# One decoder block on one core: the seven products of a 2x2 split in a form with four weight sums, made on DVE

## The chip, the cores and the metric

The kernel runs on one core of a Trainium2 chip. The metric is the device time of one execution in microseconds. Engines are named as in the profile: PE (TensorE), DVE (VectorE), ACT (ScalarE), POOL (GpSimd), and SP, which here only issues DMAs.

## The reference, cut to what matters

One layer of a hybrid decoder. The input is normalised, projected by one wide matrix, mixed by two causal token mixers, gated, projected back, added to the input and normalised again.

```python
u = _rmsnorm(h, norm_w)                              # 512 x 2048
proj = jnp.matmul(u, w_in.astype(jnp.float32))       # 2048 x 20528
(ml_q, ml_k, ml_v, ml_o, ml_z, ml_i, ml_f,
 dn_qkv, dn_z, dn_b, dn_a, gate_a, gate_b) = jnp.split(proj, idx, axis=-1)
...
h_a = h_a * jax.nn.sigmoid(ml_o) * jax.nn.silu(ml_z)
...
y_a = jnp.matmul(h_a, w_out[:ML_WIDTH])
y_b = jnp.matmul(h_b, w_out[ML_WIDTH:])
return jax.nn.sigmoid(gate_a) * y_a + jax.nn.sigmoid(gate_b) * y_b
```

The change touches only the part of `proj` for gate_b (columns 2048 to 4095 of the gates), ml_v, ml_z and ml_o: 8192 of the columns of `w_in`. All is float32.

## The kernel before, in words

**Precision.** Every float32 operand of a matmul is split into a high part (a cast to fp32r on ACT, `split_hi`, L130) and a low part (source minus high part on DVE, `split_lo`, L133). A product is three matmuls: high x high, high x low, low x high.

**Order of the work.** PE's order is the order of the program text; the other engines' instructions are put in order by the tile framework's scheduler, with priorities (`tc.high_priority`, `urgent`, `behind`). First u is normalised and transposed into `uh`, `ul` (16 tiles of 128 rows by 512 tokens). Then come the projections of one block of ML_Q and one of ML_K (`proj_cm`), then the stage of seven products, then narrow gate blocks (`narrow_gates`, whose first matmuls are L338 to L341), the units of the two mixers, wide gate blocks, and the output projection (L1217 to L1219).

**The stage of seven products.** `SEVEN` lists eight blocks: two of gates ("g"), two of ml_v ("v"), four of ml_z with ml_o ("z"). A block is a product of u with two column blocks of 512, c1 and c2. Along the 2048 rows of the weights, two neighbouring tiles of 128 form the halves of a 2x2 split, as the two halves of the tokens (256 each) and the two column blocks do; instead of eight quarter products seven are formed of sums (a scheme of Strassen's kind). Each product runs over KH = 8 pairs of tiles i, for two token tiles t, with three matmuls of 128 x 512: 7 x 8 x 2 x 3 = 336 matmuls per block.

Before, `seven` calls `group` twice. Group A does three products per i, group B four. Both add over i in banks of PSUM and at i = 7 add or copy the result into the four quarters X11, X12, X21, X22 of the SBUF tile `X` (L487, L490, L497, L498); `SINK[kind]` then applies tanh and the gates and stores from X (g_d, L531 to L538, for z blocks). `gates`, started after the stage, loads small gate rows and lets PE transpose them (L569) after POOL has cleared masks (L623) in a pool that takes over the stage's SBUF space.

**Weights.** `rplan` and `pplan` list raw tiles and prepared tiles. A raw tile is one DMA of 256 KB by SP (L216); `sum_next` makes a sum of two raw tiles (L228; the list names POOL for four of the five sums per i, DVE for one); `split_next` splits it. `next_w` is called ahead of each step of PE and keeps raw tiles, sums and splits a few steps ahead. The raw tiles of group A are loaded again for group B.

**Sums of u.** `u_sums`, started with the projection of ML_K, forms the sums of u for each i: POOL adds high and low parts (L453), then two sums (L455, L456), DVE one (L458); all are split (L462, L463) into `s5`, `s1` and `s6`.

Of the kernel before, what the change touches and what calls it, by code (L numbers as in the profile page):

```python
# [8 lines left out]
F32 = mybir.dt.float32  # L9
# [20 lines left out]
NEXTRA = 5  # L30
SUMAHEAD = 5
# [27 lines left out]
def hybrid_body(  # L59
# [80 lines left out]

    rplan, pplan = [], []

    def add_raw(w, c, k, nk, n, extra=False):
        rplan.append((w[k * P:(k + nk) * P, c:c + n], nk, n, extra))
        return len(rplan) - 1

    def add_plain(key, *raw):
        pplan.append((key, (add_raw(*raw),), None, None))

    for c in (ML_Q, ML_K):  # L150
        for k in range(0, KT, KP):
            add_plain(("i", c, k), w_in, c, k, KP, NB)
    nx = [0]

    def extra_raw(c, k):
        nx[0] += 1
        return add_raw(w_in, c, k, 1, NO, (nx[0] - 1) % (NRAW + NEXTRA) < NEXTRA)

    for kind, c1, c2 in SEVEN:
        for i in range(KH):  # L160
            r11, r22 = extra_raw(c1, 2 * i), extra_raw(c2, 2 * i + 1)
            for m, (rs_, op) in enumerate((((r11,), None), ((r22,), None), ((r11, r22), ALU.add))):
                pplan.append((("A", c1, i, m), rs_, op, G))
        for i in range(KH):
            r11, r12 = extra_raw(c1, 2 * i), extra_raw(c2, 2 * i)
            r21, r22 = extra_raw(c1, 2 * i + 1), extra_raw(c2, 2 * i + 1)
            for m, (rs_, op, e) in enumerate((((r21, r11), ALU.subtract, G), ((r12, r22), ALU.subtract, V),
                                              ((r11, r12), ALU.add, G), ((r21, r22), ALU.add, G))):
                pplan.append((("B", c1, i, m), rs_, op, e))
    def add_gates(blocks):  # L170
        for b in blocks:
            for k in range(0, KT, KP):
                add_plain(("i", GATE + b * NB, k), w_in, GATE + b * NB, k, KP, NB)

    add_gates(range(GFIRST))
    for kind, p in UNITS:
        cols = (DN_K, DN_Q, DN_V, DN_Z) if kind == "d" else (ML_Q, ML_K)
        for c in cols:
            for k in range(0, KT, KP):
                add_plain(("i", c + p * NB, k), w_in, c + p * NB, k, KP, NB)  # L180
    add_gates(range(GFIRST, GNARROW))
    for c in range(GATE + GNARROW * NB, GATE + GEND * NO, NO):
        for k in range(KT):
            add_plain(("w", c, k), w_in, c, k, 1, NO)
    for nb in range(D // NO):
        for k in range(2 * KT):
            add_plain(("o", nb * NO, k), w_out, nb * NO, k, 1, NO)

    left = [0] * len(rplan)
    for _, rs_, _, _ in pplan:  # L190
        for r in rs_:
            left[r] += 1
    raws, sums, parts = [], [], []
    held = {False: [], True: []}
    used = [0]
    extra_pool = []

    def may_load():
        r = len(raws)
        if r == len(rplan):  # L200
            return False
        extra = rplan[r][3]
        n = NEXTRA if extra else NRAW
        return len(held[extra]) < n or left[held[extra][-n]] == 0

    def load_raw():
        assert may_load()
        r = len(raws)
        src, nk, n, extra = rplan[r]
        held[extra].append(r)  # L210
        with tc.high_priority(offset=2 * PRIO if r > RAHEAD else 0):
            if extra:
                raw = extra_pool[0].tile([P, nk, n], F32, tag="wr2", name="wr", bufs=NEXTRA)
            else:
                raw = wp.tile([P, nk, n], F32, tag="wr", name="wr", bufs=NRAW)
            nc.sync.dma_start(raw, src.rearrange("(k p) n -> p k n", p=P))  # L216
        raws.append(raw)

    def sum_next():
        key, rs_, op, e = pplan[len(sums)]  # L220
        while len(raws) <= max(rs_):
            load_raw()
        if op is None:
            sums.append(None)
            return
        with tc.high_priority(offset=2 * PRIO):
            t = wp.tile([P, 1, NO], F32, tag="tg", name="ws", bufs=3)
            e.tensor_tensor(out=t, in0=raws[rs_[0]], in1=raws[rs_[1]], op=op)  # L228
        for r in rs_:
            left[r] -= 1  # L230
        sums.append(t)

    def split_next():
        i = len(parts)
        while len(sums) <= i:
            sum_next()
        src = sums[i]
        if src is None:
            r = pplan[i][1][0]
            src = raws[r]  # L240
            left[r] -= 1
        _, nk, n, _ = rplan[pplan[i][1][0]]
        with tc.high_priority(offset=2 * PRIO if i > SAHEAD else 0):
            hi = wp.tile([P, nk, n], F32R, tag="wh", name="wh", bufs=NSPL)
            lo = wp.tile([P, nk, n], F32R, tag="wl", name="wl", bufs=NSPL)
            with ExitStack() as first:
                if not parts:
                    first.enter_context(behind("V"))
                    first.enter_context(behind("A"))
                split_hi(hi, src)  # L250
                split_lo(lo, src, hi)
        parts.append((hi, lo))

    def next_w(*key):
# [1029 lines left out]
```

## Time and profile before

| | before |
|---|---|
| timed runs | 2368.11, 2370.42, 2370.58 us, median 2370.42 |
| profiled execution | 2375.3 us, its span 2373.5 us |
| mean granted TensorE clock | 0.991 |
| busy: PE, DVE, ACT, POOL | 2250.5, 1623.2, 924.4, 669.9 us |
| stage of seven products | first matmul at 86.0 us, first matmul behind it at 796.0 us |
| HBM read, written | 303.80 MB, 51.68 MB |

A row of a group reads: line, engine, operation, output and inputs by the program's names, shapes, count; then busy time, mean ns of one, and the idle time of the engine just ahead of them with what ended it. A row of the timeline reads: start, duration, engine, line, operation, and in brackets the idle time ahead of it with what ended it; "x4" means four merged instructions. A row of busy time by stretch gives the stretch, its length, and for each engine the busy time and the number of instructions, then the granted clock, the busy share of the DMA engines and their GB/s. "ps" is a PSUM bank of the stage, "wr" a raw tile, "ws" a sum of weights, "wh" and "wl" the split parts.

### The profile page before, as it was taken

To read this page: it belongs to the slowest core of one execution; us is meant where nothing else is said; L and a number is where in the kernel's file an instruction comes from. 1 tells how busy PE (TensorE), PEld (TensorE's weight loads), DVE (VectorE), ACT (ScalarE), POOL (GpSimd) and SP (SyncE) were. 2 spreads that over 40 slices of the span, in tenths; PEclk is the share of its full clock that TensorE was granted. 3 is DMA by queue.
4 is the path that set the end of the run, shared out by engine and by line. 5 is a ranking of instruction groups with operands and counts; after the bars stand their busy time and mean duration, and the time that the engine had idled before them with its cause. 6 is when DMAs were issued, how large, how long until landed. Compare 5 with 4: busy or idle time off the path is not lost.

```text
span 2373.5 us, 33466 instructions
## 1 busy us (share of the span) xinstructions
PE 2250.5 (95%) x11455; PEld 1853.5 (78%) x11455; DVE 1623.2 (68%) x2739; ACT 924.4 (39%) x1902; POOL 669.9 (28%) x573
## 2 busy tenths in 40 slices
PE   6799899999999799999999999999999999999998
PEld 5577677777777698888878888888888997888886
DVE  4998988899999748683677648683778434444334
ACT  4345444344444334433433334343443324322222
POOL 0864664564575313020221112110311000010010
PEclk9999999999999899999999999999999999999999
DMA  4345555555555465574665656574665458634433
GB/s 146 98 146 177 181 156 174 180 156 150 164 154 159 143 169 135 134 182 109 162 145 138 173 127 152 133 189 116 158 138 140 125 164 253 194 114 124 124 116 129
DMA packets 484141, 357.72 MB, mean 151 GB/s; under 512 B 236705, under 2 KB 391554, under 8 KB 483970
## 3 DMA queue, kind: packets, MB, share of 16 engines
q1 hardware_dynamic: 400258, 329.06, 50.0%
q10 hardware_dynamic: 83712, 26.52, 4.5%
q8 instruction: 90, 1.47, 0.2%
q14 instruction: 81, 0.66, 0.1%
HBM read 303.80 MB, written 51.68 MB: 150 GB/s over the span
## 4 chain that ended last, share of the span: by engine, by line
PE 57%; issue 14%; POOL 9%; DVE 8%; DMA 5%; ACT 1%; SPq 1%; ACTq 0%; POOLq 0%; DVEq 0%
PE pj L323 10%; PE pj L324 9%; PE pj L325 9%; POOL ws L228 9%; PE py L1217 5%; PE py L1219 5%; PE py L1218 5%; DVE wl L133 3%; DVE X L490 2%; PE pjt L338 2%; PE pjt L340 2%; PE pjt L341 2%; DMA wr<-in_w_in_dram 2%; PE ps L476 1%; PE ps L477 1%
## 5 line engine op out<-in xcount | busy, mean ns | idle before, releaser
L133 DVE TENSOR_TENSOR wl<-wr,wh 128x512 fp32r<-128x512 f32 x640 | 487.6, 765 | 426.6 <-ACT wh L130 407.2
L130 ACT CAST wh<-wr 128x512 fp32r<-128x512 f32 x640 | 395.6, 620 | 853.1 <-PE pj L324 345.6
L323 PE MATMUL pj<-uh,wh 128*128 128x512 f32 x1280 | 529.7, 414 | 2.2 <-ACT yp L675 1.2
L325 PE MATMUL pj<-uh,wl 128*128 128x512 f32 x1280 | 501.5, 392 | 3.1 <-DVE wl L133 3.1
L324 PE MATMUL pj<-ul,wh 128*128 128x512 f32 x1280 | 500.6, 391 | 0.3 <-DVE ul L405 0.3
L228 POOL TENSOR_TENSOR ws<-wr 128x512 f32<-128x512 f32 x256 | 410.8, 1624 | 274.2 <-DVE wl L133 266.0
L133 DVE TENSOR_TENSOR wl<-ws,wh 128x512 fp32r<-128x512 f32 x320 | 335.6, 1076 | 31.8 <-ACT wh L130 24.6
L130 ACT CAST wh<-ws 128x512 fp32r<-128x512 f32 x320 | 198.8, 621 | 279.8 <-POOL ws L228 204.4
L325 PEld LDWEIGHTS pj<-uh,wl 128*128 128x128 f32 x1280 | 240.6, 188 | 56.5 <-DVE wl L133 4.0
L323 PEld LDWEIGHTS pj<-uh,wh 128*128 128x128 f32 x1280 | 241.5, 189 | 48.9 <-ACT uh L404 1.7
L324 PEld LDWEIGHTS pj<-ul,wh 128*128 128x128 f32 x1280 | 241.7, 189 | 43.9 <-DVE ul L405 0.8
L1217 PE MATMUL py<-wh,hh 128*128 128x512 f32 x512 | 200.7, 392 | 4.2 <-ACT tgw L1177 4.2
L1218 PE MATMUL py<-wl,hh 128*128 128x512 f32 x512 | 200.1, 391 | 0.0
L1219 PE MATMUL py<-wh,hl 128*128 128x512 f32 x512 | 200.1, 391 | 0.0
L477 PE MATMUL ps<-wl,s6h 128*128 128x512 f32 x256 | 106.1, 414 | 23.6 <-DVE wl L133 23.6
L477 PE MATMUL ps<-wl,s5h 128*128 128x512 f32 x256 | 104.1, 406 | 24.4 <-DVE wl L133 24.4
L1217 PEld LDWEIGHTS py<-wh,hh 128*128 128x128 f32 x512 | 96.7, 189 | 25.6 <-ACT tgw L1177 5.8
L1241 POOL TENSOR_TENSOR hf<-hf,fw 128x512 f32<-128x512 f32 x12 | 18.6, 1572 | 336.2 <-DMA wr<-in_w_out_dram 173.2
L1219 PEld LDWEIGHTS py<-wh,hl 128*128 128x128 f32 x512 | 96.7, 189 | 20.3
L1218 PEld LDWEIGHTS py<-wl,hh 128*128 128x128 f32 x512 | 96.8, 189 | 20.0
L338 PE MATMUL pjt<-wh,uh 128*128 128x256 f32 x384 | 112.1, 292 | 0.0
L340 PE MATMUL pjt<-wl,uh 128*128 128x256 f32 x384 | 109.6, 285 | 1.2 <-DVE wl L133 1.2
(282 smaller groups left out, 3823.8 us busy)
## 6 DMA issues: line engine op xcount, KB each, us to landing
wr<-in_w_in_dram SPq DMA_DIRECT2D x768, 256.0 KB, 3.0
wr<-in_w_out_dram SPq DMA_DIRECT2D x128, 256.0 KB, 2.9
tgl<-tg_d SPq DMA_DIRECT2D x32, 256.0 KB, 3.6
xt<-in_x_dram SPq DMA_DIRECT2D x8, 512.0 KB, 8.2
tg_d<-X ACTq DMA_DIRECT2D x16, 256.0 KB, 3.5
v_d<-X ACTq DMA_DIRECT2D x16, 256.0 KB, 5.1
g_d<-X ACTq DMA_DIRECT2D x16, 256.0 KB, 2.4
v<-v_d SPq DMA_DIRECT2D x8, 512.0 KB, 6.0
```

Of the source, the lines that this page charges most:

```text
L130: newest["A"] = A.copy(hi, src).ins
L133: newest["V"] = V.tensor_tensor(out=lo, in0=src, in1=hi.bitcast(F32), op=ALU.subtract).ins
L228: e.tensor_tensor(out=t, in0=raws[rs_[0]], in1=raws[rs_[1]], op=op)
L323: T.matmul(ps[j], hi[:, k, wsl], uh[:, kt, :], start=(kt == 0), stop=False)
L324: T.matmul(ps[j], hi[:, k, wsl], ul[:, kt, :], start=False, stop=False)
L325: T.matmul(ps[j], lo[:, k, wsl], uh[:, kt, :], start=False, stop=(kt == KT - 1))
L338: T.matmul(o, uh[:, kt, tsl], hi[:, k, :], start=(kt == 0 and c % 2 == 0), stop=False, skip_group_check=True)
L340: T.matmul(o, uh[:, kt, tsl], lo[:, k, :], start=False, stop=False, skip_group_check=True)
L477: T.matmul(ps[m][t], ah, lo[:, 0, :], start=False, stop=False)
L1217: T.matmul(ps[c], hh[base][:, kt, tsl], hi[:, 0, :], start=(kt == 0), stop=False)
L1218: T.matmul(ps[c], hh[base][:, kt, tsl], lo[:, 0, :], start=False, stop=False)
L1219: T.matmul(ps[c], hl[base][:, kt, tsl], hi[:, 0, :], start=False, stop=(kt == KT - 1))
```

## The change

Another form of the seven products, with four sums of weights per pair of tiles rather than five. The work is cut into quads (`quads`): per block eight of group A, now with four products (m6, m1, m5, m7), and eight of group B, now with three (m1, m5, m7). The products of B are added into the banks in which those of A stand; only at the end of A are copies taken (U1 = m1 + m6, C22 = U1 + m5 + m7), and at the end of B come the results m1, U1 + m5, U1 + m7 and C22.

`load_quad` loads three tiles of 256 KB per quad (buffer `wr3`, three deep): three of `w_in` in A; in B two of `w_in` and one of `t2_d`, a DRAM tensor into which A's sum `ts` was stored (by ACT's queue) eight quads earlier. `prep_quad` makes the sums on DVE: in A one of 1024 columns (`t13`) and one of 512 (`ts`), in B one of 512. Two neighbouring tiles are split as one of 1024 columns (`w2h`, `w2l`, two buffers). While PE is on quad n, quad n+1 is prepared and raw tiles of quad n+3 are asked for; `lead` starts this within the projection of ML_K. The plain list `plan` knows the stage no longer; `limit` holds its prefetch back until the last quad. Results go out through `tg` (three buffers, shared with `ts`) from PSUM, or late from U1 and C22. `u_sums` makes the sum of high and low parts on DVE and POOL in turn, then four sums of 256 columns on POOL, in one buffer rather than two.

```diff
-    def sum_next():
-        key, rs_, op, e = pplan[len(sums)]
...
-        with tc.high_priority(offset=2 * PRIO):
-            t = wp.tile([P, 1, NO], F32, tag="tg", name="ws", bufs=3)
-            e.tensor_tensor(out=t, in0=raws[rs_[0]], in1=raws[rs_[1]], op=op)
...
-    s5h, s5l = (sap.tile([P, KH, S], F32R, tag=f"s5{n}", name=f"s5{n}") for n in "hl")
-    s1h, s1l = (sap.tile([P, KH, HP], F32R, tag=f"s1{n}", name=f"s1{n}") for n in "hl")
+    suh, sul = (sap.tile([P, KH, 3, HP], F32R, tag=f"su{n}", name=f"su{n}") for n in "hl")
...
     def u_sums():
         for i in range(KH):
...
-            G.tensor_tensor(out=uf, in0=uh[:, 2 * i:2 * i + 2, :].bitcast(F32), in1=ul[:, 2 * i:2 * i + 2, :].bitcast(F32),
+            uf, sf = X[:, 0, :, :], X[:, 1, :, :].rearrange("p a (b n) -> p (a b) n", n=HP)
+            E = V if i % 2 == 0 else G
+            E.tensor_tensor(out=uf, in0=uh[:, 2 * i:2 * i + 2, :].bitcast(F32), in1=ul[:, 2 * i:2 * i + 2, :].bitcast(F32),
                             op=ALU.add)
...
+            a11, a21, a12, a22 = uf[:, 0, 0:HP], uf[:, 0, HP:S], uf[:, 1, 0:HP], uf[:, 1, HP:S]
+            G.tensor_tensor(out=sf[:, 0], in0=a21, in1=a22, op=ALU.add)
+            G.tensor_tensor(out=sf[:, 1], in0=sf[:, 0], in1=a11, op=ALU.subtract)
+            G.tensor_tensor(out=sf[:, 2], in0=a11, in1=a21, op=ALU.subtract)
+            G.tensor_tensor(out=sf[:, 3], in0=a12, in1=sf[:, 1], op=ALU.subtract)
             yield 1
+            for hi, lo, src in ((suh[:, i], sul[:, i], sf[:, 0:3]), (s4h[:, i], s4l[:, i], sf[:, 3])):
                 A.copy(hi, src)
                 V.tensor_tensor(out=lo, in0=src, in1=hi.bitcast(F32), op=ALU.subtract)
             yield 1
...
+    def load_quad():
...
+        with tc.high_priority(offset=2 * PRIO):
+            r = sbp.tile([P, 3, NO], F32, tag="wr3", name="wr3", bufs=3)
+            k1, k2 = (slice((2 * i + n) * P, (2 * i + n + 1) * P) for n in range(2))
+            if g == "A":
+                src = (w_in[k1, c1:c1 + NO], w_in[k1, c2:c2 + NO], w_in[k2, c2:c2 + NO])
+            else:
+                src = (w_in[k2, c1:c1 + NO], w_in[k2, c2:c2 + NO], t2_d[b % 2, i])
+            for n in range(3):
+                nc.sync.dma_start(r[:, n, :], src[n])
+        rawq.append(r)
...
+    def prep_quad():
...
+        def split(src, wide):
+            if wide:
+                hi, lo = (sbp.tile([P, 2, NO], F32R, tag=f"w2{n}", name=f"w{n}", bufs=2) for n in "hl")
+            else:
+                hi, lo = (wp.tile([P, 1, NO], F32R, tag=f"w{n}", name=f"w{n}", bufs=NSPL) for n in "hl")
+            split_hi(hi, src)
+            split_lo(lo, src, hi)
+            return [(hi[:, n, :], lo[:, n, :]) for n in range(2 if wide else 1)]
+
+        with tc.high_priority(offset=2 * PRIO):
+            ts = wp.tile([P, 1, NO], F32, tag="tg", name="ts", bufs=3)
+            if g == "A":
+
+                t13 = sbp.tile([P, 2, NO], F32, tag="t13", name="t13")
+                V.tensor_tensor(out=t13, in0=r[:, 1:3, :], in1=r[:, 0:2, :], op=ALU.subtract)
+                V.tensor_tensor(out=ts[:, 0, :], in0=r[:, 2, :], in1=t13[:, 0, :], op=ALU.subtract)
+                w6 = split(ts, False)
+                nc.scalar.dma_start(t2_d[b % 2, i], ts[:, 0, :])
+                p_ = w6 + split(r[:, 0:1, :], False) + split(t13, True)
+            else:
+
+                V.tensor_tensor(out=ts[:, 0, :], in0=r[:, 0, :], in1=r[:, 2, :], op=ALU.subtract)
+                p_ = split(r[:, 0:2, :], True) + split(ts, False)
+        partq.append(p_)
...
+    LHS = {"A": (lambda i, t: (suh[:, i, 1, t], sul[:, i, 1, t]),
+                 lambda i, t: (uh[:, 2 * i, t], ul[:, 2 * i, t]),
+                 lambda i, t: (suh[:, i, 0, t], sul[:, i, 0, t]),
+                 lambda i, t: (suh[:, i, 2, t], sul[:, i, 2, t])),
+           "B": (lambda i, t: (uh[:, 2 * i + 1, t], ul[:, 2 * i + 1, t]),
+                 lambda i, t: (s4h[:, i, t], s4l[:, i, t]),
+                 lambda i, t: (uh[:, 2 * i + 1, half2(t)], ul[:, 2 * i + 1, half2(t)]))}
...
+    def seven(n0, kind, c1, c2):
+
+        m6, m1, m5, m7 = ([pool.tile([P, NO], F32, tag=t, name="ps") for pool, t in banks_] for banks_ in (OO, JW, JW, JW))
+        ends = {"A": (None, lambda t: (copy1(t, m1[t]), add(U1[t], U1[t], m6[t])),
+                      lambda t: add(C22[t], U1[t], m5[t]), lambda t: add(C22[t], C22[t], m7[t])),
+                "B": SINK[kind](c1, c2, m1, m5, m7)}
+        for n in range(2 * KH):
+            g, i = "AB"[n // KH], n % KH
+            prep_quad()
+            load_quad()
+            if n0 + n == len(quads) - 1:
+                limit[0] = len(plan)
+                prepare(nfront - 1)
+            for m, ps in enumerate((m6, m1, m5, m7) if g == "A" else (m1, m5, m7)):
+                hi, lo = partq[n0 + n][m]
+                for t in range(2):
+                    ah, al = LHS[g][m](i, slice(t * P, (t + 1) * P))
+                    T.matmul(ps[t], ah, hi, start=(g == "A" and i == 0), stop=False, skip_group_check=True)
+                    T.matmul(ps[t], ah, lo, start=False, stop=False, skip_group_check=True)
+                    T.matmul(ps[t], al, hi, start=False, stop=(i == KH - 1), skip_group_check=True)
+                    if i == KH - 1 and ends[g][m] is not None:
+                        ends[g][m](t)
+                tick()
...
+    def sink_flat(dst, func, scale):
+
+        def sink(c1, c2, m1, m5, m7):
+            def out_(ps, c, col):
+                o = wp.tile([P, NO], F32, tag="tg", name="to", bufs=3)
+                with urgent(3):
+                    A.activation(o, ps, func, scale=scale)
+                nc.scalar.dma_start(dst(c, col), o)
...
+            def end5(t):
+                add(m5[t], U1[t], m5[t])
+                out_(m5[t], t, c2)
+                start(late(C22[t], 2 + t, c2), 1)
+
+            def end7(t):
+                add(U1[t], U1[t], m7[t])
+                start(late(U1[t], 2 + t, c1), 2)
...
+    def sink_z(c1, c2, m1, m5, m7):
...
+        def late(t):
+            th = wp.tile([P, NO], F32, tag="tg", name="to", bufs=3)
+            with behind("A"):
+                A.activation(th, U1[t], AF.Tanh, scale=0.5)
+                A.activation(C22[t], C22[t], AF.Tanh, scale=0.5)
+            with behind("V"):
+                V.scalar_tensor_tensor(out=U1[t], in0=th, scalar=1.0, in1=U1[t], op0=ALU.add, op1=ALU.mult)
+            V.scalar_tensor_tensor(out=U1[t], in0=C22[t], scalar=1.0, in1=U1[t], op0=ALU.add, op1=ALU.mult)
+            yield 2
+            with behind("A"):
+                nc.scalar.dma_start(g_d[2 + t, :, col:col + NO], U1[t])
+
+        def end7(t):
+            add(U1[t], U1[t], m7[t])
+            start(late(t), 3 + 2 * t)
...
+    def lead(kt):
+        if kt in (7, 9, 11):
+            load_quad()
+        if kt == 13:
+            prep_quad()
...
-    spill(proj_cm(ML_K), 2, 1.0)
-    for blk in SEVEN:
-        seven(*blk)
+    spill(proj_cm(ML_K, before=lead), 2, 1.0)
+    for b, blk in enumerate(SEVEN):
+        seven(2 * KH * b, *blk)
```

242 lines of the change are left out of this document (77 added, 165 removed).

## The prediction

> **What bounds the kernel now.** I read the page first (busy time, chain, groups), then who PE waited for, then the busy time by stretch.
>
> ```profile
> PE 2250.5 (95%) x11455; PEld 1853.5 (78%) x11455; DVE 1623.2 (68%) x2739; ACT 924.4 (39%) x1902; POOL 669.9 (28%) x573
> ...
> PE 57%; issue 14%; POOL 9%; DVE 8%; DMA 5%; ACT 1%; SPq 1%; ACTq 0%; POOLq 0%; DVEq 0%
> ...
> L228 POOL TENSOR_TENSOR ws<-wr 128x512 f32<-128x512 f32 x256 | 410.8, 1624 | 274.2 <-DVE wl L133 266.0
> L133 DVE TENSOR_TENSOR wl<-ws,wh 128x512 fp32r<-128x512 f32 x320 | 335.6, 1076 | 31.8 <-ACT wh L130 24.6
> ...
> PE ps L477 <- DVE wl L133: 51.4, 72, 2.8
> ...
> PE ps L476 <- DVE X L490: 8.8, 12, 1.1
> ```
>
> PE counts as busy for 95% of the span, yet POOL holds 9% of the chain, and POOL's main work is the sums of weights (L228). PE's longest wait is for the low parts of split weights (wl, L133), and those made from sums take 1076 ns. For the adds that combine products (L490) it waits 8.8 us in all.
>
> ```profile
> core 0: us, PE busy (x) PEld busy (x) DVE busy (x) ACT busy (x) POOL busy (x), PEclk, DMA share, GB/s
> 60.60:86.00 25.40, 22.26 (x97) 17.53 (x95) 22.22 (x14) 7.93 (x16) 23.96 (x14) 1.00 0.44 134
> 86.00:139.40 53.40, 39.01 (x144) 27.90 (x144) 52.49 (x51) 25.32 (x49) 35.31 (x22) 0.90 0.32 91
> ...
> 190.20:226.10 35.90, 33.28 (x143) 26.63 (x144) 26.25 (x35) 20.28 (x35) 10.74 (x8) 1.00 0.61 185
> 226.10:276.40 50.30, 46.47 (x195) 35.51 (x193) 49.27 (x47) 20.49 (x34) 39.77 (x25) 1.00 0.52 161
> ```
> ```profile
> L476 PE MATMUL ps<-wh,s5h x256: 387/389/796, 86.0 to 745.2; 128*128 128x512 f32 x128
> L338 PE MATMUL pjt<-wh,uh x384: 276/283/560, 796.0 to 1961.9; 128*128 128x256 f32 x192
> 225.81 1.29 DVE L487 TENSOR_TENSOR X<-ps,X 128x512 f32<-128x512 f32 x2 [0.75 <-PE ps L478]
> 312.01 1.29 DVE L487 TENSOR_TENSOR X<-ps,X 128x512 f32<-128x512 f32 x2 [0.75 <-PE ps L478]
> 659.83 1.29 DVE L487 TENSOR_TENSOR X<-ps,X 128x512 f32<-128x512 f32 x2 [0.75 <-PE ps L478]
> 746.78 1.29 DVE L487 TENSOR_TENSOR X<-ps,X 128x512 f32<-128x512 f32 x2 [0.75 <-PE ps L478]
> 2199.69 0.39 PE L1219 MATMUL py<-wh,hl 128*128 128x512 f32 x1
> 2205.81 0.39 PE L1219 MATMUL py<-wh,hl 128*128 128x512 f32 x1
> ```
>
> The stage of seven products runs from its first matmul at 86.0 to the first narrow gate matmul at 796.0: 710.0 us for eight blocks. L487 comes once per block, at the end of group A, so a block takes 312.01 - 225.81 = 86.2 us, and 746.78 - 659.83 = 87.0 where it is a z block. PE's own pace is seen in the output stage, where nothing is waited for: 27 matmuls start in 2205.81 - 2199.69 = 6.12 us, 0.2267 us each. A block has 7 x 8 x 2 x 3 = 336, so 76.2 us at that pace, and 10 to 11 us are lost. Group A (144 matmuls, 32.6 us) takes 35.9, group B (192, 43.5 us) takes 50.3. In group B DVE is busy for 49.27 of 50.30 us with only 47 instructions, 1.05 us each. The first group A is worst: 53.4 us, with DVE busy for 52.49 of them.
>
> ```profile
> 304.54 0.69 DVE L228 TENSOR_TENSOR ws<-wr 128x512 f32<-128x512 f32 x1
> 308.67 1.29 POOL L228 TENSOR_TENSOR ws<-wr 128x512 f32<-128x512 f32 x1 [6.87 <-DVE wl L133]
> 326.96 1.67 DVE L228 TENSOR_TENSOR ws<-wr 128x512 f32<-128x512 f32 x1
> 799.09 0.68 DVE L133 TENSOR_TENSOR wl<-wr,wh 128x512 fp32r<-128x512 f32 x1
> 799.69 0.67 DVE L490 TENSOR_TENSOR X<-X,ps 128x512 f32<-128x512 f32 x1
> L389 DVE SCALAR_TENSOR_TENSOR jv<-xt x4: 1216/1221/1226, 6.1 to 15.7; 128x1024 f32<-128x1024 f32 x4
> ```
>
> The same sum on DVE takes 0.69 us while POOL is idle and 1.67 beside a POOL sum. So the bound is neither engine's work alone: POOL and DVE slow each other, and the low parts come late. Undisturbed, DVE starts a 512-wide operation every 799.69 - 799.09 = 0.60 us.
>
> **Weight preparation in the steady blocks (2 to 8).** The change takes the sums from POOL, so all DVE work is priced undisturbed: 0.60 us for 512 columns. No two-tensor sum of 1024 columns is in the trace; the nearest row is L389, 1.22 us, less the 0.08 overlap that a 512-wide one shows (0.68 against 0.60), so 1.14 (bounds 0.60 and 1.20). A quad of group A: t13 1.14, ts 0.60, three low parts 0.60 + 0.60 + 1.14, together 4.08 us, beside 24 matmuls of 0.2267 = 5.44. A quad of group B: 1.14 + 0.60 + 0.60 = 2.34, beside 18 matmuls = 4.08. Per block 8 x 6.42 = 51.4. The combination of products falls from 16 DVE operations to 10, 6.0 us; a z block keeps its eight for the gates, 4.8. DVE needs 57 to 62 us of 76.2, and PE becomes the bound.
>
> ```profile
> L130 ACT CAST wh<-wr 128x512 fp32r<-128x512 f32 x640 | 395.6, 620 | 853.1 <-PE pj L324 345.6 <-PE py L1219 207.8 <-PE ps L478 76.9
> 61.17 0.40 ACTq L438 DMA_DIRECT2D gr_d<-gr  x1
> wr<-in_w_in_dram SPq DMA_DIRECT2D x768, 256.0 KB, 3.0
> v_d<-X ACTq DMA_DIRECT2D x16, 256.0 KB, 5.1
> 1950.00:2010.00 60.00, 57.66 (x302) 49.21 (x301) 24.31 (x35) 24.38 (x39) 0.00 (x0) 1.00 0.82 259
> ```
>
> ACT's share of a group A quad is four times 512 columns, at most 4 x 0.62 = 2.48, and 0.40 for issuing the new store of t2: under 5.44, with the low parts a quad ahead as cover. SP still issues 48 loads per block (24 + 24 for 16 + 32), eight of them from t2_d. Each of those follows its store by eight quads, some 38 us, against 5.1 + 3.0 us for a slow store and a load; without that distance each would cost about 8 us. Traffic per block is 48 loads, 8 stores of t2 and 8 of results, 64 x 0.262 = 16.8 MB in 77.7 us, 216 GB/s. Between 1950 and 2010 us the trace shows 259 GB/s with PE busy for 57.66 of 60, so I charge nothing.
>
> Nothing hides the hand-overs fully. One set of three bank pairs carries both groups. At the end of A, six DVE adds (3.6 us) and two ACT copies must be through before m5 and m7 are accumulated further; m7's bank pair has 12 matmuls, 2.7 us, until then, and the DVE is only three quarters full. At the end of B the last results pass through the tg ring of three buffers, which ts shares; a fourth user waits until the first store has landed (5.1 us in the v row), and ACT and DVE issue in order behind it. Bounds: 0, if the quad of lead (4 to 5 us) covers it, and 5 us. I take 1.5, nearer to zero, because 16 such adds per block cost PE 8.8 us over eight blocks today. Block: 77.7 us.
>
> **The first block.** POOL still does the activation sums here, four operations of 256 columns and every second sum of 1024.
>
> ```profile
> L453 POOL TENSOR_TENSOR X<-uh,ul 128x1024 f32<-128x1024 f32 x8 | 21.1, 2646 | 45.0 <-PE pgr L415 42.4 <-DVE s6f L458 2.6
> L228 POOL TENSOR_TENSOR ws<-wr 128x512 f32<-128x512 f32 x11 | 17.6, 1599 | 14.9 <-DVE wl L133 14.9
> L455 POOL TENSOR_TENSOR X<-X 128x512 f32<-128x512 f32 x8 | 12.8, 1604 | 2.0 <-DVE s5l L463 2.0
> L456 POOL TENSOR_TENSOR X<-X 128x256 f32<-128x256 f32 x8 | 9.2, 1145 | 0.0
> 84.79 2.39 POOL L453 TENSOR_TENSOR X<-uh,ul 128x1024 f32<-128x1024 f32 x1 [0.69 <-DVE s6f L458]
> 117.13 0.91 POOL L456 TENSOR_TENSOR X<-X 128x256 f32<-128x256 f32 x1
> ```
>
> I add the undisturbed work of both engines from 60.6 us to the end of the first group A and compare it with the clock. Before: DVE 14 + 51 instructions, 57 at 0.60 and eight of 256 columns at 0.33 (0.60 less half of the step to 1.14), 36.8 us; POOL 8 x 2.39 + 19 x 1.29 + 8 x 0.91 = 50.9; together 87.7 in 78.8 us, a ratio of 0.90. (Group B: 47 x 0.60 + 25 x 1.29 = 60.5 in 50.3, ratio 0.83.) After: DVE has 6 splits of K (3.6), four sums (4.6), eight low parts of 768 and of 256 columns (0.87 + 0.33, 9.6), eight quads of A, the first of them within the projection of K, and one of B (32.6 + 2.3), 52.7; POOL 4 x 2.39 + 32 x 0.91 = 38.7. Together 91.4, times 0.90 is 82.3, so group A ends at 142.9; group B adds 144 x 0.2267 = 32.6. First block: 142.9 + 32.6 - 86.0 = 89.5 us. Bounds: 76.2 (PE's pace) and, with a ratio of 1, 98.6.
>
> [...]
>
> **The end of the stage.**
>
> ```profile
> 806.29 2.48 DVE L535 SCALAR_TENSOR_TENSOR X<-X 128x512 f32<-128x512 f32 x4
> 811.28 0.22 ACT L600 ACTIVATE sml<-bia 128x16 f32<-128x16 f32 x1 [6.06 <-DMA g_d<-X]
> 814.71 0.98 PE L569 MATMUL pgt<-ident,gr 112*128 112x112 f32 x4 [12.84 <-POOL msk L623]
> ```
>
> PE stands for 12.84 us until the last results have left X and POOL has cleared its masks in the space. DVE's part ends at 808.8, 12.8 after the stage. After the change two tiles are left rather than four: one late add (0.7), four tanh beside four DVE operations (4 x 0.6, and one tanh ahead, 0.6), some 4 us, then the same store and clearing (814.71 - 808.8 = 5.9): PE resumes about 11 us after the stage, not 18.7. Bounds 0 and 8; I take 6. The first weights of the next stage are loaded only in the last quad (3.0 us load, 1.3 split, 4.08 us of cover), within this idle stretch in any case.
>
> **Sum.** 710.0 - (89.5 + 7 x 77.7 = 633.4) = 76.6, plus 6, gives 82.6. The profiled execution took 2375.3 us (span 2373.5); it becomes 2292.7. The three timed runs lie lower, median 2370.4, by 4.9, so I forecast **2288**.
>
> **Rivals.** (1) The hand-overs cost 7 us per block rather than 1.5: the stage saves 38 us less, about 2326. For it: DVE, ACT and the tg ring all serve both weights and results. Against it: the adds of L490 cost PE 1.1 us per block now. 0.13.
> (2) Slower: the lead is lost. Each raw triple has three buffers, freed only by the preparation, and SP issues in order, so one late t2 load holds back the w_in loads behind it. If load and preparation fall in series, a B quad takes 3.0 + 0.60 + 0.62 + 0.60 = 4.8 and handshakes of some 0.2, 0.9 over PE's 4.08; an A quad 3.0 + 1.14 + 0.60 + 0.62 + 0.60 and the same, 6.2 to 6.6, up to 1.1 over. That is 16 us per block, 92: 89.5 + 7 x 92 = 733.5, less the 6 of the end, 17 us slower, 2388. It decides from (716 - 89.5)/7 = 89.5 us per block, 13.3 over PE's pace, 0.83 us per quad. Against it: loads are two quads ahead, about 9 us, for 3.0 us of transfer. 0.10.
> (3) The change does not relieve DVE, because its 1.05 us in group B are not POOL's doing. Then a block needs (51.4 + 8)/0.60 x 1.05 = 104 us, the stage 832, some 2490. Against it: 0.69 for the same operation with POOL idle. 0.04.
>
> **How the numbers follow.** My case holds 0.70: from 76.2 us in every block and 8 us at the end (2262) to 99 in the first and 79 in the rest (2307). Rival 1 reaches from there to 2335; its rest and the two slower rivals are left out. Range 2262 to 2335. A measurement of this kernel tells about 0.2% from no change. Faster 0.83 (my case and rival 1), same 0.03 (between rivals 1 and 2), slower 0.14.
>
> **What would show it.** In the profile after: no POOL sums between about 140 us and the end of the stage; low parts of 512 columns at about 0.68 us and of 1024 at 1.2; DVE busy for 75 to 85% of a steady block; blocks of 76 to 79 us; a first group A that still ends near 140 us with DVE full; PE's idle time ahead of the pgt transposes down to about 6 us. I am wrong if PE's waits for wl or for adds keep their sum, if ACT waits for stores of t2 or of results, or if the granted clock falls in the denser stage.

## The result, and the profile after

| | before | after |
|---|---|---|
| median | 2369.27 us (2366.14 to 2370.58) | 2302.6 us (2301.78 to 2304.38) |
| ratio, 95% interval | | 0.9722 [0.9705, 0.9738] |
| profiled execution, its span | 2375.3, 2373.5 us | 2304.38, 2302.6 us |
| stage of seven products | 86.0 to 796.0 | 81.6 to 737.3 |
| PE resumes behind the stage | 814.7 | 750.9 |

The kernel is 2.8% faster: 2302.6 us, where 2288 with a range of 2262 to 2335 was forecast. First the page of the kernel after: busy time and chain.

```profile
PE 2229.2 (97%) x11455; PEld 1857.8 (81%) x11455; DVE 1483.9 (64%) x2679; ACT 884.8 (38%) x1758; POOL 263.8 (11%) x329
...
PE 78%; DVE 8%; DMA 8%; issue 3%; ACT 2%; SPq 1%; POOL 0%; DVEq 0%; ACTq 0%; POOLq 0%
```

What PE waited for (us in total, times, longest):

```profile
PE ps L473 <- DVE wl L131: 13.0, 9, 2.8
PE pgt L584 <- POOL xi L809: 9.2, 1, 9.2
PE ps L472 <- ACT to L490: 7.7, 6, 2.1
PE ps L472 <- DVE X L449: 5.7, 8, 1.3
```

POOL has left the chain (9% before, 0% now) and PE holds 78% of it (57% before). PE's wait for low parts falls from 51.4 us to 13.0, all of it ahead of 140 us, in the first group A. The wait for adds (now L449) falls from 8.8 to 5.7. A new one stands beside it: 7.7 us for ACT's copies of results out of the banks (`to`, L490). These are the groups of the weight preparation, different shapes apart:

```profile
L131 DVE TENSOR_TENSOR wl<-ts,wh 128x512 fp32r<-128x512 f32 x128 | 92.2, 725 | 18.4 <-ACT wh L128 17.8
L131 DVE TENSOR_TENSOR wl<-t,wh 128x1024 fp32r<-128x1024 f32 x64 | 81.5, 1274 | 40.8 <-ACT wh L128 40.7
L423 DVE TENSOR_TENSOR t<-wr 128x1024 f32<-128x1024 f32 x64 | 80.0, 1250 | 5.2 <-DMA wr<-in_w_in_dram 4.7
L430 DVE TENSOR_TENSOR ts<-wr 128x512 f32<-128x512 f32 x64 | 44.1, 690 | 49.1 <-DMA wr<-t_d 48.7 <-issue 0.2
```

A low part of a sum, 1076 ns before, takes 725 at 512 columns (the first block, with POOL at work, is in that mean), and 1274 for two of them in one instruction. The time by stretch, the first group A up to its first copy out of the banks and the last steady block:

```profile
core 0: us, PE busy (x) PEld busy (x) DVE busy (x) ACT busy (x) POOL busy (x), PEclk, DMA share, GB/s
81.60:140.30 58.70, 45.58 (x181) 33.88 (x180) 55.42 (x53) 24.35 (x38) 32.13 (x24) 0.97 0.45 144
622.81:701.13 78.32, 77.29 (x337) 62.76 (x336) 64.45 (x83) 35.52 (x50) 0.00 (x0) 1.00 0.62 203
```

DVE is still full in this part of the first group A (55.42 of 58.70 us) and busy for 82% of a steady z block, with POOL idle. The ends of the stage, from the answers by source line (durations, then first and last start):

```profile
L472 PE MATMUL ps<-wh,suh x384: 388/389/632, 81.6 to 703.7; 128*128 128x512 f32 x192
L256 PE MATMUL pjt<-wh,uh x384: 277/283/562, 737.3 to 1891.5; 128*128 128x256 f32 x192
```

A mark near the end of group A, in four of the eight blocks, from the timeline (L453, the first copy out of the banks), and below it the first matmul of group B in the first and in the last block:

```profile
140.32 1.07 ACT L453 COPY X<-ps 128x512 f32<-128x512 f32 x2
220.09 1.27 ACT L453 COPY X<-ps 128x512 f32<-128x512 f32 x2 [0.98 <-PE ps L474]
301.03 1.27 ACT L453 COPY X<-ps 128x512 f32<-128x512 f32 x2 [0.63 <-PE ps L474]
701.13 1.27 ACT L453 COPY X<-ps 128x512 f32<-128x512 f32 x2 [0.98 <-PE ps L474]
143.03 0.39 PE L472 MATMUL ps<-wh,uh 128*128 128x512 f32 x1
704.33 0.39 PE L472 MATMUL ps<-wh,uh 128*128 128x512 f32 x1
```

The mark stands where m1 is complete, with the 12 matmuls of m5 and m7 still to come: the first group A ends at 143.0 us, 2.7 behind its mark, and takes 61.5 us; the last group B takes 33.0 (704.33 to 737.3). From mark to mark the seven steady blocks take 79.8, 80.9, 82.2, 81.9, 78.4, 79.3 and 78.3 us, 80.1 in the mean (86.8 before; 76.2 at PE's pace). The g and v blocks lose more than the z blocks, and three rows of the timeline say where, at the end of the first group B:

```profile
182.08 0.60 ACT L490 ACTIVATE to<-ps 128x512 f32<-128x512 f32 x1 [2.41 <-DMA tg_d<-to]
182.71 0.69 DVE L424 TENSOR_TENSOR ts<-wr,t 128x512 f32<-128x512 f32 x1 [2.73 <-DMA tg_d<-to]
182.73 0.50 PE L472 MATMUL ps<-wh,suh 128*128 128x512 f32 x1 [1.88 <-ACT to L490]
```

ACT's copy stood for 2.41 us until the store of an earlier result had landed and its buffer of the ring `tg` was free; DVE's `ts` stood for 2.73 us for the same; PE then waited 1.88 us for the bank that ACT had not yet emptied.

So the span's 70.9 us divide into four: the stage begins 4.4 us earlier (86.0 - 81.6), is 54.3 shorter (710.0 - 655.7), PE resumes behind it after 13.6 us rather than 18.7 (5.1), and everything behind that takes 1551.7 us rather than 1558.8 (7.1).

### The profile page after: what moved, and what is told of

The parts are those of the page before. It is cut to its first block, busy times and chain, and to the rows that moved or that the text cites. A ratio compares the mean times of both kernels' runs of the same rounds, so it can differ in the third digit from the quotient of the medians.

```text
span 2302.6 us, 32600 instructions
## 1 busy us (share of the span) xinstructions
PE 2229.2 (97%) x11455; PEld 1857.8 (81%) x11455; DVE 1483.9 (64%) x2679; ACT 884.8 (38%) x1758; POOL 263.8 (11%) x329
## 4 chain that ended last, share of the span: by engine, by line
PE 78%; DVE 8%; DMA 8%; issue 3%; ACT 2%; SPq 1%; POOL 0%; DVEq 0%; ACTq 0%; POOLq 0%
PE pj L241 12%; PE pj L242 12%; PE pj L243 12%; PE ps L472 5%; PE ps L473 5%; PE py L1232 5%; PE ps L474 5%; PE py L1234 5%; PE py L1233 5%; DVE wl L131 3%; PE pjt L256 2%; DMA wr<-in_w_in_dram 2%; PE pjt L259 2%; PE pjt L258 2%; DMA wr<-t_d 1%
## 5 line engine op out<-in xcount | busy, mean ns | idle before, releaser
L131 DVE TENSOR_TENSOR wl<-wr,wh 128x512 fp32r<-128x512 f32 (+1 forms) x640 | 499.2, 783 | 422.3 <-ACT wh L128 400.2
L128 ACT CAST wh<-wr 128x512 fp32r<-128x512 f32 (+1 forms) x640 | 423.8, 663 | 814.3 <-PE pj L242 355.3
L472 PE MATMUL ps<-wh,suh 128*128 128x512 f32 x384 | 153.2, 399 | 11.5 <-ACT to L490 7.7
L473 PE MATMUL ps<-wl,suh 128*128 128x512 f32 x384 | 152.3, 397 | 6.5 <-DVE wl L131 6.5
L473 PE MATMUL ps<-wl,uh 128*128 128x512 f32 x384 | 151.6, 395 | 6.6 <-DVE wl L131 6.5
L472 PE MATMUL ps<-wh,uh 128*128 128x512 f32 x384 | 150.6, 392 | 2.0 <-DVE X L449 1.5
L474 PE MATMUL ps<-wh,sul 128*128 128x512 f32 x384 | 151.4, 394 | 0.0
L474 PE MATMUL ps<-wh,ul 128*128 128x512 f32 x384 | 150.1, 391 | 0.0
L128 ACT CAST wh<-ts 128x512 fp32r<-128x512 f32 x128 | 79.2, 619 | 141.1 <-DVE ts L430 98.2
L128 ACT CAST wh<-t 128x1024 fp32r<-128x1024 f32 x64 | 67.3, 1052 | 147.1 <-DVE ts L424 60.3
```

The source lines that it names most:

```text
L128: newest["A"] = A.copy(hi, src).ins
L131: newest["V"] = V.tensor_tensor(out=lo, in0=src, in1=hi.bitcast(F32), op=ALU.subtract).ins
L472: T.matmul(ps[t], ah, hi, start=(g == "A" and i == 0), stop=False, skip_group_check=True)
L473: T.matmul(ps[t], ah, lo, start=False, stop=False, skip_group_check=True)
L474: T.matmul(ps[t], al, hi, start=False, stop=(i == KH - 1), skip_group_check=True)
```

## The experiments

Ratios are to the kernel before on the same chip. The theory, A, was that POOL and DVE slow each other: who makes the sums matters most, the form less. The rivals were that the form itself (fewer sums, wide pairs, fewer adds) saves the time, and, for what is left of the loss, three candidates: activation sums, the ring `tg`, the trip of t2 through DRAM.

**e1: the old form, its sums on DVE.** In the kernel before, all five sums go to DVE.

```diff
-                pplan.append((("A", c1, i, m), rs_, op, G))
+                pplan.append((("A", c1, i, m), rs_, op, V))
-            for m, (rs_, op, e) in enumerate((((r21, r11), ALU.subtract, G), ((r12, r22), ALU.subtract, V),
-                                              ((r11, r12), ALU.add, G), ((r21, r22), ALU.add, G))):
+            for m, (rs_, op, e) in enumerate((((r21, r11), ALU.subtract, V), ((r12, r22), ALU.subtract, V),
+                                              ((r11, r12), ALU.add, V), ((r21, r22), ALU.add, V))):
```

> The kernel before with its five weight sums per pair of tiles all on DVE and nothing else changed. Theory A (the gain comes from taking the sums off POOL, whatever the form): an old B quad has 8 DVE operations, 4.8 us beside 5.44 us of PE, an old A quad 4, 2.4 us beside 4.08; steady blocks of 78 to 81 us rather than 86 to 87, the first group A some 6 us shorter, about 2317 us (2305 to 2330). Theory B (the gain comes from the form: four sums, spread more evenly, made and split in pairs): DVE is still too full in the B quads and the time stays above 2345 us.

Measured: 2329.31 us, ratio 0.9832 [0.9817, 0.9848]. Groups by shape in one steady block:

```profile
L133 DVE TENSOR_TENSOR wl<-ws,wh 128x512 fp32r<-128x512 f32 x40 | 27.3, 687 | 5.9 <-ACT wh L130 5.6
L228 DVE TENSOR_TENSOR ws<-wr 128x512 f32<-128x512 f32 x40 | 26.6, 686 | 0.4
```

That block in the busy time by stretch:

```profile
217.30:300.00 82.70, 79.81 (x338) 64.76 (x337) 70.62 (x113) 41.02 (x70) 0.00 (x0) 0.96 0.57 178
```

PE's waits in the whole run:

```profile
PE ps L477 <- DVE wl L133: 16.1, 14, 2.6
PE ps L476 <- DVE X L490: 12.6, 13, 1.7
```

All forty sums of a block are on DVE now, 32 of them from POOL, and DVE is no longer full: 70.62 of 82.70 us. Before, it was busy for 75.5 of 86.2 us (26.25 and 49.27, the rows from 190.20 to 276.40 us in the prediction) with 82 instructions; now it has 113 and is busy for less. Its low parts fall from 1076 to 687 ns, because POOL has stopped. Of the 67 us, 40 come from the engine alone. The blocks settle at 82.1 us (the seven lie between 80.5 and 82.7), still 5.9 over PE's pace though DVE has room; PE waits for low parts and adds, and its granted clock is 0.96 in this block.

**e2: the new form, its sums on POOL.** In the kernel after, t13 and both `ts` go to POOL.

```diff
-                V.tensor_tensor(out=t13, in0=r[:, 1:3, :], in1=r[:, 0:2, :], op=ALU.subtract)
-                V.tensor_tensor(out=ts[:, 0, :], in0=r[:, 2, :], in1=t13[:, 0, :], op=ALU.subtract)
+                G.tensor_tensor(out=t13, in0=r[:, 1:3, :], in1=r[:, 0:2, :], op=ALU.subtract)
+                G.tensor_tensor(out=ts[:, 0, :], in0=r[:, 2, :], in1=t13[:, 0, :], op=ALU.subtract)
...
-                V.tensor_tensor(out=ts[:, 0, :], in0=r[:, 0, :], in1=r[:, 2, :], op=ALU.subtract)
+                G.tensor_tensor(out=ts[:, 0, :], in0=r[:, 0, :], in1=r[:, 2, :], op=ALU.subtract)
```

> The changed kernel with its weight sums on POOL rather than DVE. Theory A (POOL and DVE stand in each other's way): an A quad has 3.7 us of POOL and 2.3 us of DVE, which take 5.0 to 6.0 us together beside 5.44 of PE, and the low parts stretch to over 1 us per 512 columns; steady blocks of 81 to 87 us, 2315 to 2355 us in all. Theory B (the form decides, not the engine): within 5 us of 2303.

Measured: 2379.68 us, ratio 1.0043 [1.003, 1.0055], slower than the kernel before and worse than either theory had it. Groups by shape in one steady block (244.0 to 331.8 us):

```profile
L423 POOL TENSOR_TENSOR t<-wr 128x1024 f32<-128x1024 f32 x8 | 20.7, 2591 | 14.7 <-DVE wl L131 14.7
L131 DVE TENSOR_TENSOR wl<-wr,wh 128x512 fp32r<-128x512 f32 x8 | 17.5, 2190 | 0.0
```

PE's largest wait in the stage, over the whole run:

```profile
PE ps L473 <- DVE wl L131: 44.9, 30, 4.5
```

The low part of the raw tile in A, 512 wide, takes 2190 ns, three times its 0.69, and POOL's wide sum 2591; the block takes 87.8 us, and the wait for low parts is back at 44.9 us. With e1 this makes a table of medians:

| sums made on | POOL | DVE |
|---|---|---|
| old form | 2369.3 | 2329.3 |
| new form | 2379.7 | 2302.6 |

The form alone, on POOL, loses 10 us; on DVE it gains 27. The engine alone gains 40 in the old form and 77 in the new. "Form" stands here for all of the change but the engine: four sums, wide pairs, the lead, products added in the banks. Both theories hold a part: the two halves of the change need each other.

**e3: the activation sums on DVE too.** In the kernel after, POOL's last work in the first block goes.

```diff
-            E = V if i % 2 == 0 else G
+            E = V
...
-            G.tensor_tensor(out=sf[:, 0], in0=a21, in1=a22, op=ALU.add)
+            V.tensor_tensor(out=sf[:, 0], in0=a21, in1=a22, op=ALU.add)
...
```

> The changed kernel with the sums of u all on DVE. If the first block is held up by POOL and DVE working beside each other: the first group A ends at 127 to 132 us rather than 140.3, PE's waits for wl in it nearly vanish, about 2292 us. Rival (it is the chain of the sums of u through one buffer, or DVE's own work): within 3 us of 2303, or a little slower, since DVE gets more to do.

Measured: 2303.09 us, ratio 0.9726 [0.9711, 0.974], the same as after. The first group A by stretch:

```profile
81.90:132.70 50.80, 44.07 (x182) 33.91 (x181) 50.00 (x76) 23.75 (x38) 0.00 (x0) 0.98 0.58 176
```

Its end, from the timeline:

```profile
132.74 1.06 ACT L453 COPY X<-ps 128x512 f32<-128x512 f32 x2
```

A wait of PE:

```profile
PE ps L472 <- ACT to L490: 9.1, 6, 2.8
```

DVE does more (76 instructions, not 53) in less time, and the group ends 7.6 us earlier. It is then DVE's own work that fills it, 50.00 of 50.80 us. But the gain does not reach the end: the four g and v blocks take 82.9, 82.0, 82.7 and 82.0 us (81.2 in the mean after), with 9.1 us of waits for `to`; PE resumes at 747.8, only 3.1 us earlier, and the rest behind is 2.7 us longer. So the theory was right about the first group A and wrong about the time; the rival's number came true, but because the blocks behind gave the gain back.

**e4: `ts` out of the ring.** `ts` is written over the third raw tile, which it consumes, instead of taking a buffer of `tg`.

```diff
-            ts = wp.tile([P, 1, NO], F32, tag="tg", name="ts", bufs=3)
+            ts = r[:, 2:3, :]
```

> The changed kernel with ts written over the third raw tile rather than into the tg ring, so that results alone use the ring. If the ring causes the loss at the hand-overs (ACT waits 2 us for a store of a result, PE waits for ACT): steady g and v blocks fall from 80 to 82 us to 78 or 79, z blocks by under 1, about 2294 us (2288 to 2298). Rival (the fourth result still waits for the store of the first, so ACT waits as before, and raw tiles come free later): within 3 us of 2303.

Measured: 2313.91 us, ratio 0.9772 [0.9758, 0.9787], 11 us slower than after. A miss. PE's waits in the stage:

```profile
PE ps L473 <- DVE wl L131: 11.8, 8, 3.1
PE ps L472 <- DVE X L449: 10.9, 18, 1.8
PE ps L472 <- ACT to L490: 8.2, 5, 2.3
```

The wait for `to` stays (8.2): with three buffers the fourth result waits for the first one's store whether `ts` takes part or not. The wait for adds rises to 10.9. The raw tile now has to be kept until the t2 store from it has landed, and that holds the loads back. What SP waits for between 140 and 705 us shows it:

```profile
SPq L400 <- DMA t_d<-wr: 227.3, 55, 7.6
```

In the kernel after SP does not wait for these stores at all. DVE's wait for the t2 tiles grows from 42.8 to 58.6 us in the same stretch, and the steady blocks take 81.5 us in the mean rather than 80.1. That the late loads make all of the 11 us is not shown.

**e5: two results fewer in the ring.** C22 is complete at the end of A. It is stored from there, in g and v blocks, eight quads before the end; m5's result then goes to C22's place in X rather than to `tg`.

```diff
-                      lambda t: add(C22[t], U1[t], m5[t]), lambda t: add(C22[t], C22[t], m7[t])),
+                      lambda t: add(C22[t], U1[t], m5[t]), lambda t: (add(C22[t], C22[t], m7[t]), early(t))),
...
-                out_(m5[t], t, c2)
-                start(late(C22[t], 2 + t, c2), 1)
+                with urgent(3):
+                    A.activation(C22[t], m5[t], func, scale=scale)
+                nc.scalar.dma_start(dst(t, c2), C22[t])
```

(`early` is `start(late(C22[t], 2 + t, c2), 2 + 2 * t)` for g and v, nothing for z.)

> The changed kernel, where in g and v blocks C22 is stored at the end of group A, when it is complete, and its place in X takes the results of m5, so that the tg ring has two results per block rather than four. If the ring causes the hand-over loss of these blocks: ACT no longer waits for a store ahead of them, PE's waits for ACT there (7.7 us) and the slow matmuls behind them vanish, the blocks of 80 to 82 us become 77 to 79, about 2292 us (2288 to 2296). Rival (ACT or DVE is late through its own load there): within 3 us of 2303.

Measured: 2290.64 us, ratio 0.9684 [0.9667, 0.97]. PE's largest wait behind the first group A:

```profile
PE ps L474 <- DVE X L449: 5.1, 7, 1.3
```

A steady block by stretch:

```profile
216.90:294.00 77.10, 76.98 (x337) 62.88 (x336) 59.66 (x75) 35.30 (x51) 0.00 (x0) 1.00 0.67 215
```

Its two marks on the timeline:

```profile
216.88 1.27 ACT L453 COPY X<-ps 128x512 f32<-128x512 f32 x2 [0.98 <-PE ps L476]
294.00 1.27 ACT L453 COPY X<-ps 128x512 f32<-128x512 f32 x2 [0.99 <-PE ps L476]
```

There is no wait for `to` any more. The same block took 80.9 us after and takes 77.1 here, with PE busy for 76.98. The g and v blocks are now the fast ones (77.1 to 78.4; z 78.4 to 78.9). So the ring was the hand-overs' main cost in g and v blocks. The edit also takes two stores and, in g blocks, ACT's pass over C22 away from that place; what they cost there is not told apart from the ring. By medians the gain over the kernel after is 12 us, by ratios (the runs are from different chips) 9.

**e6: e5 and e3 together.** The edits of both.

> The same with the sums of u all on DVE. In the kernel with these sums alone the first group A ended 7.6 us earlier, and the next four blocks gave it back with longer hand-overs. If those were the ring's: 6 to 8 us below the kernel with C22 stored early, about 2285 us. Rival (what is gained ahead is given back by whatever comes next): within 2 us of that kernel.

Measured: 2282.22 us, ratio 0.9650 [0.9635, 0.9664], the fastest kernel here. One steady block by stretch:

```profile
210.50:287.30 76.80, 76.67 (x337) 62.90 (x336) 59.47 (x75) 35.16 (x50) 0.00 (x0) 1.00 0.67 215
```

The first matmul behind the stage (716.2), by source line:

```profile
L256 PE MATMUL pjt<-wh,uh x384: 277/284/561, 716.2 to 1869.1; 128*128 128x256 f32 x192
```

What e3 could not keep is kept here: the first group A ends 6.5 us earlier than in e5, the stage 6.7, and the median is 8.4 lower; what does not show in the stage lies behind it, where no cause was found. The same edit is worth nothing with the ring in the way and about 7 us of the stage without it.

**e7: the pairs undone.** Both the wide sum and the wide splits become two of 512 columns.

```diff
-            split_hi(hi, src)
-            split_lo(lo, src, hi)
+            for n in range(2 if wide else 1):
+                split_hi(hi[:, n, :], src[:, n, :])
+                split_lo(lo[:, n, :], src[:, n, :], hi[:, n, :])
...
-                V.tensor_tensor(out=t13, in0=r[:, 1:3, :], in1=r[:, 0:2, :], op=ALU.subtract)
+                for k in range(2):
+                    V.tensor_tensor(out=t13[:, k, :], in0=r[:, k + 1, :], in1=r[:, k, :], op=ALU.subtract)
```

> The changed kernel with each pair summed and split as two operations of 512 columns rather than one of 1024, in the same tiles. Theory (pairs save only the fixed part of an operation): DVE gets 3 x 0.06 us per two quads more, PE does not notice, within 4 us of 2303. Rival (pairs are part of the gain): over 10 us slower.

Measured: 2321.63 us, ratio 0.9812 [0.9798, 0.9827], 19 us slower than after by medians, 21 by ratios: the theory missed, its rival was right. PE's waits behind the first group A:

```profile
PE ps L474 <- ACT to L492: 7.7, 4, 3.1
PE ps L474 <- DVE to L530: 4.6, 6, 1.3
PE ps L475 <- DVE wl L131: 4.0, 4, 1.4
```

One hand-over on the timeline:

```profile
434.79 0.60 ACT L492 ACTIVATE to<-ps 128x512 f32<-128x512 f32 x1 [1.97 <-DMA v_d<-to]
435.44 0.74 PE L474 MATMUL ps<-wh,suh 128*128 128x512 f32 x1 [3.06 <-ACT to L492]
```

The first group A takes 63.1 us to its mark rather than 58.7, the steady blocks 81.7 in the mean rather than 80.1. In these PE's longest wait for `to` grows from 2.1 to 3.1 us, low parts are waited for again (none after), and the z blocks' gates (L530) hold PE up for 4.6 us, where it was 0.3 after.

**e8: no trip of t2 through DRAM.** B loads a tile of `w_in` in place of t2, and A's store is dropped; the bytes loaded are the same, but `ts` of B is then formed of other data.

```diff
-                src = (w_in[k2, c1:c1 + NO], w_in[k2, c2:c2 + NO], t2_d[b % 2, i])
+                src = (w_in[k2, c1:c1 + NO], w_in[k2, c2:c2 + NO], w_in[k1, c1:c1 + NO])
...
-                nc.scalar.dma_start(t2_d[b % 2, i], ts[:, 0, :])
```

> The changed kernel where group B loads a tile of w_in in place of t2 and group A does not store t2: the way through HBM is left out, and ts of group B is computed from other data. Theory (store and load are hidden by the eight quads between them): within 4 us of 2303, though DVE waits 48.7 us in all for the t2 loads. Rival (these waits reach PE): 2285 to 2295.

Measured: 2300.69 us, ratio 0.9725 [0.9711, 0.974]. DVE's sum in B, by shape:

```profile
L429 DVE TENSOR_TENSOR ts<-wr 128x512 f32<-128x512 f32 x64 | 44.1, 689 | 48.4 <-DMA wr<-in_w_in_dram 48.4
```

The trip costs nothing that can be told. DVE stood for 48.7 us in all for t2's loads in the kernel after (L430, above), and it stands for 48.4 here for a plain tile of `w_in` in the same place: the wait was for the last load of a quad, not for the trip, and it is idle time of an engine with room.

**e9 and e10: the pairs undone on top of e5.** e9 has the edits of e5 and e7; e10 those of e5 and only the sum t13 as two.

> The kernel with C22 stored early, its pairs undone: each is summed and split as two operations of 512 columns. Undoing the pairs cost 19 us in the changed kernel. If it cost them because longer queues met the tg ring's waits at the hand-overs: within 5 us of 2291. If the more numerous operations cost time by themselves, in the first group A (about 5 us there) and at every hand-over (12 us over seven blocks): 2303 to 2312.

> The kernel with C22 stored early, where only the sum t13 is made as two operations of 512 columns; the pairs are still split as one. It adds 64 DVE operations, 0.06 us each beyond the columns, and nothing on ACT. If only the undisturbed DVE price counts: within 3 us of 2291. If the splits are what the pairs gain from, the same; if the number of DVE operations is, about half of what undoing all pairs costs.

Measured: e9 2299.28 us, 0.9703 [0.9686, 0.9719]; e10 2299.16 us, 0.9699 [0.9685, 0.9714]. By ratios they lie 4.5 and 3.6 us above e5, by medians (from different chips) 8.6 and 8.5. In the traces the stage is 5.0 and 5.5 us longer than in e5. Where the ring is relieved, the pairs are thus worth 4 to 9 us rather than 19: at least half of e7's loss came only with the ring in the way. What is left shows at the ends of z blocks (in e9 also in the first group A, 3.3 us to its mark), in e9 first, then in e10:

```profile
PE ps L476 <- DVE to L533: 4.6, 6, 1.3
```
```profile
PE ps L475 <- DVE to L532: 3.2, 6, 0.8
```

The two intervals and that of e5 overlap, so this loss is not clear of the noise by ratios. That e10, with the sum alone undone, is as slow as e9 points to the sum, but does not settle it.

## Why the prediction was right, and where its terms were off

The profiled execution was forecast at 2292.7 us and took 2304.38, 11.7 more. The terms, in the order of the sum:

- **Who bounds: right.** That POOL and DVE slow each other, and that DVE alone has room, is shown by e1 (687 ns against 1076 for the same low part, 40 us) and by e2 (2190 ns). Rival 3, that 1.05 us was DVE's own time, fell with e1.
- **Prices on DVE: right.** A wide sum was taken at 1.14 us between starts; 1.25 of duration less the 0.08 of overlap is 1.17. A g or v block was to keep DVE busy for 57 us and does for 59.7 (e5's row, and the same between the marks at 220.09 and 301.03 here); a z block for 62, and does for 64.45.
- **Hand-overs: the term that was mis-sized.** 1.5 us per block was taken from bounds of 0 and 5, because the adds cost little before. It is 4.0: from the end of the first group A to that of the last (143.0 to 704.3) a block takes 80.2 us, not 77.7, which makes 17.4 us over seven blocks. The prediction named the very cause, a fourth user of the ring behind a store, but priced it by the adds' row. It listed ACT's waits for stores of results among the signs of being wrong, and that sign came; e5 prices it at 9 to 12 us. Rival 1 was right in kind and too high in size (7 us). The waits of PE for `to` and X, 13.4 us, are only half of what is lost; three stretches of 3.4 to 4.0 us in which PE's granted clock is 0.50, 0.53 and 0.62 (last section) lose, by an estimate from their rows (9 or 10 matmuls where 15 or 16 would start at 0.2267 us each), some 4 to 5 more. The rest is mostly single matmuls that start 0.1 us or more late at full clock, beside these waits: about 8 us by their starts in the trace, and about 7 in e5.
- **First group A: its end right, partly by luck.** It was to end at 142.9 and did at 143.0. The stage began 4.4 us earlier, which was not forecast (the projection of ML_K no longer waits: PE is busy for all 21.00 us from 60.6 to 81.6), but this brought nothing, as the group is through when DVE and POOL are: it took 61.5 us rather than 56.9.

```profile
60.60:81.60 21.00, 21.00 (x94) 17.19 (x92) 18.38 (x16) 8.62 (x14) 14.97 (x13) 1.00 0.69 224
61.33 0.74 POOL L375 TENSOR_TENSOR X<-X 128x256 f32<-128x256 f32 x1 [43.39 <-DVE X L372]
```

From 60.6 to 143.0 are 82.4 us for the 91.4 of both engines' undisturbed work, the ratio of 0.90 that was taken. But 0.91 us for a POOL sum of 256 columns was not undisturbed: DVE worked beside the row that the prediction took it from, and where DVE stands (61.1 to 63.1 us) such a sum takes 0.74. With 0.74 the work is 86.0 us, the ratio comes out at 0.96, and the prediction's own sum would have ended the group at about 139. The prediction's bound, a ratio of 1 (the two engines' work one after the other), would, by an estimate from the same rows, have put the end at 152.0 with 0.91 (60.6 + 91.4) and at 146.6 with 0.74 (60.6 + 86.0); the trace has 143.0. So the two engines gained less from working beside each other than the prediction held, 4% of their work rather than 10%, and e2's low part of 2190 ns, 0.69 us undisturbed, shows how strong the interference is.
- **t2 and the lead: right.** e8 shows the trip at nothing, and no PE wait for a low part is left behind the first block; rival 2 did not come about. The 0.2 us of handshakes in its sum was an estimate for four of them; single ones in the trace before take 0.03 to 0.08 us:

```profile
94.85 1.22 DVE L133 TENSOR_TENSOR wl<-ws,wh 128x512 fp32r<-128x512 f32 x1
96.12 0.51 PE L477 MATMUL ps<-wl,s1h 128*128 128x512 f32 x1 [0.47 <-DVE wl L133]
96.15 3.08 POOL L228 TENSOR_TENSOR ws<-wr 128x512 f32<-128x512 f32 x2 [0.63 <-DVE wl L133]
96.33 1.77 DVE L458 TENSOR_TENSOR s6f<-X 128x512 f32<-128x512 f32 x1
98.13 0.62 ACT L462 CAST s6h<-s6f 128x512 fp32r<-128x512 f32 x1 [4.32 <-DVE s6f L458]
```

- **End of the stage: nearly right.** 6 us were forecast, 5.1 came; PE stands for 9.16 us instead of 12.84, where about 6 was expected.
- **The last group B: right.** It takes 33.0 us where 32.6 was forecast.
- **Behind the stage: not forecast.** 7.1 us less, in small steps over the mixers' units and once before the output. In the other kernels this part takes 1549 to 1557 us, without an order that follows one edit. Its cause stays open.

In sum: 17.4 + 0.4 too little for the stage behind the first group A, 0.1 for that group's end and 0.9 for the end of the stage, less 7.1 that came unforeseen, makes the 11.7. The 7.1 were luck: without them the median would have been about 2309.7, still in the range but above 2307, where the prediction's own case ended, and the steady blocks of 80.2 us lie above that case's 79 in any event. The 1.8 us between this run and its median, where 4.9 were taken over from before, is the rest of the way from 2288 to 2302.6.

## What to carry to other kernels

That two engines slow each other was seen here in the mean duration of the same instruction beside and without the other (a low part: 1076 ns before, 687 in e1); when one of them is emptied, price the work that moves at the undisturbed duration, and take that from a row beside which the other engine stands (0.74 us for a POOL sum of 256 columns, not 0.91). The ring of buffers that both results and operands use tied the operands to the landing of stores (`ts` stood for 2.73 us at 182.71): much of what remained after the bound engine was relieved sat at such hand-overs (9 to 12 us by e5), so price them by a store's landing (5.1 us for v_d before), not by the add beside them (1.1 us per block before). A gain ahead of the stalled ring (7.6 us in e3) was given back there, and was kept once the ring was relieved (6.7 us of the stage in e6).

## What the hardware showed unexpectedly

Three short stalls of PE cost more than their length: behind them its granted clock was 0.50 to 0.62. Four hand-overs of the kernel after, by stretch:

```profile
182.00:186.00 4.00, 3.27 (x13) 2.40 (x14) 3.26 (x5) 2.31 (x5) 0.00 (x0) 1.00 0.72 278
262.00:266.00 4.00, 3.65 (x10) 2.88 (x11) 3.32 (x5) 2.18 (x5) 0.00 (x0) 0.62 0.63 233
344.60:348.10 3.50, 3.49 (x9) 2.74 (x10) 3.47 (x5) 1.40 (x3) 0.00 (x0) 0.53 0.66 254
426.80:430.20 3.40, 3.40 (x9) 2.62 (x9) 3.37 (x5) 1.45 (x3) 0.00 (x0) 0.50 0.62 238
```

The matmul that ended the third's stall, from the timeline:

```profile
344.61 0.62 PE L472 MATMUL ps<-wh,suh 128*128 128x512 f32 x1 [1.43 <-ACT to L490]
```

After idle 1.43 us, PE ran nine matmuls in 3.5 us at a granted clock of 0.53, some 0.4 us each where it starts one every 0.2267 us elsewhere, and was back at 1.00 behind that (348.40 to 352.00 us). The stall of 1.88 us at 182.73 had no such effect (clock 1.00), the one at 262.35 did, after 2.14 us (0.62), and the fourth, at 426.53 after 1.67 us (0.50). A stall of 1.31 us, at 585.31, had none either (clock 1.00). In the three, PE starts a matmul every 0.42 us or so for 3.39 us (262.92 to 266.31) and 3.75 us (344.61 to 348.36, 426.53 to 430.28), then every 0.23 again. The length of a stall alone does not tell it here: the clock fell behind 1.43 us and not behind 1.88. What sets it off, and why the stall of 1.88 us passed unharmed, stays open.
